# Two waves of Strassen products for 18 of the 25 column tiles of a decoder's input projection

## The chip, the cores and the metric

The kernel runs on one core of a Trainium2 chip. The metric is the device time in microseconds (us) of one execution, the median of several. A core has five engines that run side by side and wait for one another by semaphores: TensorE (PE, matmuls out of SBUF into the eight banks of PSUM), VectorE (DVE), ScalarE (ACT), GpSimd (POOL, which works on SBUF only) and SyncE (SP, which issues the transfers here).

## The reference

Two layers, for 1024 tokens of width 1024. Each layer is `h + mixer(norm(h))`, then `h + cross_attention(norm(h))`. The mixer begins with one projection of all tokens:

```
proj = xn @ w_in                 # (1024 x 1024) @ (1024 x 3168)
(gq, gk, gv, glr, ggate, cc, cb, ch, cgate, cq, ckv, kr, mgate) = split(proj)
o_gla  = rms_norm(gla_chunked(gq, gk, gv, log_a(glr)), gla_norm) * silu(ggate)
o_conv = cb * causal_conv3(cc * ch, conv_w) * silu(cgate)
q, k, v from rms_norm(cq) @ w_uq, rms_norm(ckv) @ w_ukv, rope(kr)
o_mla  = causal_attention(q, k, v) * silu(mgate)
return concat(o_gla, o_conv, o_mla) @ w_out
```

Everything is float32.

## The kernel before

Activations lie transposed: features on the partitions, tokens along the free dimension, in two halves c = 0, 1 of 512 tokens. So x is 8 (k) x 2 (c) tiles of 128 x 512. A float32 matmul is made of three in a shorter format: each operand is split into hi (a rounded cast, on ScalarE) and lo (the difference, on GpSimd or VectorE), and `mm3` (L298) adds hi x hi, hi x lo and lo x hi into one bank. `split` (L154) does that for activations, `wsplit` (L123) for weights; the subtraction of both is `sub` (L148), so all of them have the line L149 in the profile. `absorb` (L274) makes the parts of x as the layer before ends, and stores h in DRAM (`hd`).

`w_in` is cut into 25 tiles of 128 columns: 0 to 6 carry gq, gk and gv, 7 to 9 ggate, 10 to 17 the two halves of the conv (cc, ch, cb, cgate each), 18 and 19 cq, 20 and 21 ckv, 22 to 24 mgate. `win` (L393) loads one tile (512 KB), splits it, and for each half of the tokens makes 8 x 3 matmuls into one PSUM bank (`proj`, L305); VectorE multiplies the bank by `R`, the reciprocal norm of the tokens, into SBUF (L402). Gate tiles go through `silu` (L405) and to DRAM.

Memory is taken from pools of tagged buffers. The tag "s" has 64 granules of 128 x 512 float32, "pt" 4 and "p" 9; raw weight tiles ("wr") have 2 buffers, split ones ("w") 6. PSUM's eight banks are four with the tag S, two t, one mm and one v.

The kernel is written as generators that are advanced in a hand-made order (`layers`, L1143). A planner then simulates the engines and orders each queue: of what is ready and has its buffers it takes what was traced first. So the traced order is a priority, and work traced later can run earlier. Transfers all go through SyncE's one queue, in order. In a layer: tiles 0, 1, 2, 5 and 6 (gq, gk and the first v); `gla_front` (decays, L458) woven with the other v tiles and the first mgate; `v_tokens` (transposes of v, L443); `gla_body` (the recurrence) filled with the gates and the first conv; then ckv, cq, the second conv, rope and the attention; `out_proj`; the cross-attention.

Of the kernel before, what the change touches and what calls it, by code (L numbers as in the profile page):

```python
# [18 lines left out]
P = 128  # L19
# [41 lines left out]
def run(g):  # L61
# [4 lines left out]
BUFS = {"s": 64, "p": 9, "pt": 4, "tq": 1}  # L66
# [14 lines left out]
    "wk": (0, 2), "wv": (0, 2), "wq": (0, 2),  # L81
}


class Trunk:
# [330 lines left out]
    def gate(self, l, i, dram, name):  # L416

        gs = []

        def dst(c):  # L420
            gs.append(self.g(f"{name}_{c}", tag="pt"))
            return gs[-1]

        n = 0
        for _ in self.win(l, i, name, dst, PAIR[name[:2]]):
            self.silu(gs[n], f"{name}s_{n}")
            self.nc.sync.dma_start(dram[n], gs[n])
            n += 1
            yield

# [195 lines left out]
    def conv(self, l, j):  # L626
        nc = self.nc
        base = 10 + 4 * j
        tags = PAIR[f"conv{j}"]
        u = self.g2(f"cc{l}_{j}")  # L630
        y = self.g2(f"cy{l}_{j}")
        self.cy[j] = y
        yield from self.win(l, base, f"cc{l}_{j}", lambda c: u[c], tags)
        tmp = {}

        def dst(name):
            def f(c):
                tmp[c] = self.g(f"{name}{l}_{j}_{c}", tag="pt")
                return tmp[c]
            return f  # L640

        w = [self.gain(l, "conv", 2 * k + j) for k in range(3)]
        c = 0
        for _ in self.win(l, base + 1, f"ch{l}_{j}", dst("ch"), tags):
            self.mul(nc.gpsimd, u[c], u[c], tmp[c])
            nc.scalar.activation(y[c], u[c], AF.Copy, scale=w[2])
            for s in (1, 2):
                nc.vector.scalar_tensor_tensor(
                    y[c][:, s:], u[c][:, : 512 - s], w[2 - s], y[c][:, s:], op0=ALU.mult, op1=ALU.add
                )  # L650
                if c == 1:
                    nc.vector.scalar_tensor_tensor(
                        y[1][:, :s], u[0][:, 512 - s :], w[2 - s], y[1][:, :s], op0=ALU.mult, op1=ALU.add
                    )
            c += 1
            yield
        c = 0
        for _ in self.win(l, base + 3, f"cg{l}_{j}", dst("cg"), tags):
            self.silu(tmp[c], f"cgs{l}_{j}_{c}")
            self.mul(nc.gpsimd, y[c], y[c], tmp[c])  # L660
            c += 1
            yield
        c = 0
# [757 lines left out]
```

## Time and profile before

| | before |
|---|---|
| median of 3 runs (us) | 1416.54 (1415.16 to 1416.78) |
| profiled execution (us) | 1415.69 |
| its span, first to last instruction (us) | 1413.9 |
| granted TensorE clock, mean | 0.997 |
| busy: TensorE, VectorE, ScalarE, GpSimd (us) | 1382.9, 771.0, 690.0, 571.7 |
| moved by DMA | 131.13 MB, 93 GB/s on average |

The span is 1.8 us shorter than the time of that execution. Busy times are sums over instructions; those of one engine that overlap are counted once. A matmul's recorded time is longer than the distance to the next, since matmuls are pipelined: what one costs is read from the distance of their starts.

### The profile page before, as it was taken

How to read it: one execution, taken by the hardware profiler on the slowest of the kernel's cores; microseconds unless marked ns; L12 is line 12 of the kernel's file. 1: busy time of each engine (PE TensorE's matmuls, PEld its weight loads, DVE VectorE, ACT ScalarE, POOL GpSimd, SP SyncE). 2: the span in 40 equal slices, each digit the busy share in tenths (PEclk: the TensorE clock that was granted, in tenths of full speed). 3: DMA queues.
4: the chain of work that ended last, by engine and by line, in shares of the span. 5: the costliest groups of instructions: out<-in, count | busy, mean ns of one | idle time of the engine just before them, and what ended most of it. 6: DMA issues, size and time to landing. Idle time of an engine off the chain costs nothing.

```text
span 1413.9 us, 19744 instructions
## 1 busy us (share of the span) xinstructions
PE 1382.9 (98%) x7132; PEld 1128.0 (80%) x7132; DVE 771.0 (55%) x1431; ACT 690.0 (49%) x1462; POOL 571.7 (40%) x584
## 2 busy tenths in 40 slices
PE   7998999999999999999999999999999999999998
PEld 6787888888776688888878788888887767888886
DVE  7846445364788554545653632534657883553533
ACT  5446544253777442555431653424557773344543
POOL 6325335215556452353342532441356663414320
PEclk9999999999999999999999999999999999999999
DMA  8131222122122254321522121211232123534403
GB/s 310 53 129 53 77 76 74 47 63 91 45 61 65 92 172 134 121 89 46 185 100 82 49 78 53 89 58 45 83 86 60 33 81 112 194 105 142 156 1 120
DMA packets 61827, 131.13 MB, mean 93 GB/s; under 512 B 7553, under 2 KB 14497, under 8 KB 61729
## 3 DMA queue, kind: packets, MB, share of 16 engines
q1 hardware_dynamic: 61728, 129.87, 28.5%
q8 instruction: 56, 0.92, 0.3%
q14 instruction: 43, 0.34, 0.1%
HBM read 95.76 MB, written 33.55 MB: 91 GB/s over the span
## 4 chain that ended last, share of the span: by engine, by line
PE 83%; DVE 9%; ACT 3%; issue 2%; DMA 2%; POOL 1%; SPq 0%; DVEq 0%; POOLq 0%; ACTq 0%
PE op_ps L301 4%; PE op_ps L302 4%; PE op_ps L303 4%; PE av L848 4%; PE pt L834 3%; PE xqps L301 2%; PE xqps L302 2%; PE xqps L303 2%; PE s L301 2%; PE gg_ps L301 2%; PE gg_ps L303 2%; PE gg_ps L302 2%; PE s L303 1%; PE s L302 1%; DVE gla_a L479 1%
## 5 line engine op out<-in xcount | busy, mean ns | idle before, releaser
L149 POOL TENSOR_TENSOR win_l<-win_r,win_h 128x512 fp32r<-128x512 f32 x76 | 104.1, 1391 | 196.4 <-ACT win_h L127 191.6
L805 POOL TENSOR_SCALAR p<-p,sm 128x128 f32<-128x128 f32 (+3 forms) x144 | 87.8, 619 | 63.8 <-DVE sm L803 41.5
L127 ACT CAST win_h<-win_r 128x1024 fp32r<-128x1024 f32 x50 | 52.4, 1049 | 123.5 <-PE gg_ps L302 36.6
L303 PE MATMUL op_ps<-mix_h,wout_l 128*128 128x512 f32 x256 | 99.9, 390 | 0.0
L302 PE MATMUL op_ps<-mix_l,wout_h 128*128 128x512 f32 x256 | 99.8, 390 | 0.0
L301 PE MATMUL op_ps<-mix_h,wout_h 128*128 128x512 f32 x256 | 99.0, 393 | 0.0
L799 ACT ACTIVATE p<-s,nm 128x128 f32<-128x128 f32 (+3 forms) x144 | 83.2, 581 | 27.1 <-DVE nm L795 13.8
L791 DVE TENSOR_REDUCE nm<-s 128x1 f32<-128x128 f32 (+3 forms) x144 | 78.4, 551 | 3.1 <-PE s L303 1.1
L834 PE MATMUL pt<-ident,p 128*128 128x128 f32 x432 | 70.6, 280 | 1.6 <-POOL p L805 1.5
L834 PEld LDWEIGHTS pt<-ident,p 128*128 128x128 f32 x432 | 49.7, 140 | 27.3 <-issue 13.7
L848 PE MATMUL av<-ph,V 128*64 128x256 f32 x480 | 69.6, 375 | 0.0
L149 POOL TENSOR_TENSOR wout_l<-wout_r,wout_h 128x512 fp32r<-128x512 f32 x32 | 43.3, 1376 | 42.5 <-ACT wout_h L127 34.4
L301 PE MATMUL s<-k_h,q_h 128*128 128x128 f32 (+3 forms) x144 | 55.2, 386 | 1.3 <-ACT p L799 0.6
L301 PEld LDWEIGHTS op_ps<-mix_h,wout_h 128*128 128x128 f32 x256 | 47.7, 188 | 10.5 <-issue 0.8
L302 PEld LDWEIGHTS op_ps<-mix_l,wout_h 128*128 128x128 f32 x256 | 48.1, 188 | 9.9
L303 PEld LDWEIGHTS op_ps<-mix_h,wout_l 128*128 128x128 f32 x256 | 48.1, 188 | 9.8
L842 ACT COPY ph<-pt 128x512 f32<-128x512 f32 (+1 forms) x72 | 39.6, 549 | 23.7 <-PE pt L834 20.6
L301 PE MATMUL xqps<-op_x_h,wq_h 128*128 128x512 f32 x128 | 51.1, 399 | 0.0
L1005 POOL TENSOR_SCALAR xp<-xp,xsm 128x256 f32<-128x256 f32 x64 | 29.8, 482 | 51.4 <-DVE xsm L1003 51.3
L303 PE MATMUL xqps<-op_x_h,wq_l 128*128 128x512 f32 x128 | 50.4, 393 | 0.0
L302 PE MATMUL xqps<-op_x_l,wq_h 128*128 128x512 f32 x128 | 50.2, 392 | 0.0
L302 PE MATMUL s<-k_l,q_h 128*128 128x128 f32 (+3 forms) x144 | 49.9, 347 | 0.0
(502 smaller groups left out, 4292.5 us busy)
## 6 DMA issues: line engine op xcount, KB each, us to landing
win_r<-in_w_in SPq DMA_DIRECT2D x50, 512.0 KB, 3.6
wout_r<-in_w_out SPq DMA_DIRECT2D x16, 512.0 KB, 4.0
x<-in_x SPq DMA_DIRECT2D x16, 256.0 KB, 6.3
hd<-h SPq DMA_DIRECT2D x16, 256.0 KB, 4.0
op0r<-hd SPq DMA_DIRECT2D x16, 256.0 KB, 4.0
hd<-op0r SPq DMA_DIRECT2D x16, 256.0 KB, 2.9
wq_r<-in_w_mem SPq DMA_DIRECT2D x8, 512.0 KB, 3.8
wk_r<-in_w_mem SPq DMA_DIRECT2D x8, 512.0 KB, 3.6
```

The source lines that it names most:

```text
L127: ins = self.nc.scalar.copy(hi, raw)
L149: eng.tensor_tensor(lo, src, hi.bitcast(F32), op=ALU.subtract)
L301: nc.tensor.matmul(ps, a[0], b[0], start=first, stop=False, **k)
L302: nc.tensor.matmul(ps, a[0], b[1], start=False, stop=False, **k)
L303: nc.tensor.matmul(ps, a[1], b[0], start=False, stop=last, **k)
L791: nc.vector.tensor_reduce(nm[:, b : b + 1], ps[:, :w], axis=AX.X, op=ALU.max, negate=True)
L799: nc.scalar.activation(x[:, :w], ps[:, :w], AF.Exp, bias=nm[:, 0:1], accum_out=sm[:, b : b + 1])
L805: nc.gpsimd.tensor_scalar(pr[b][:, :w], pr[b][:, :w], sm[:, 0:1], 1.0, op0=ALU.mult, op1=ALU.mult)
L834: nc.tensor.transpose(ps[:, o : o + P], prob[qi][kt // 4][:, (kt % 4) * P : (kt % 4 + 1) * P], self.ident,)
L842: nc.scalar.copy(pt[:, :w], ps[:, :w])
L848: nc.tensor.matmul(av[own if j == 0 else other, q0:256], self.V[kt][:, 64 * h : 64 * h + 64], pt[:, j * 256 : j * 256 + 256 - q0], start=( ...
L1005: nc.gpsimd.tensor_scalar(pr[:, j], pr[:, j], sm[:, j : j + 1], 1.0, op0=ALU.mult, op1=ALU.mult)
```

## The change

18 of the 25 tiles of a layer are projected in nine pairs. With x cut into four quarters (the halves of the tokens by the halves of k, `half(j, c)`) and a pair of weight tiles cut into four as well, Strassen's method in Winograd's form gives the four quarters of the result from seven products of 4 x 3 matmuls in place of eight. It needs four sums of quarters of x (`a_side`: made anew from the stored h, the gains and R, stored in DRAM, later loaded and split by `s_parts`) and four of the weights (`w_first`, `w_second`). Wave one makes three products per pair with the x parts as they are, and stores two of the results (`pd`) and one weight sum (`wtd`); wave two makes the other four with the sums of x, and adds up. The parts of x are given up after wave one, and the sums take their place. The gate results of the conv go through DRAM too (`cgd`), the latents and the convs take their inputs from what wave two leaves (`Sink`, `GateSink`), and the order in `layers` is new. "s" has 58 granules, "pt" 6, and there are 4 raw weight buffers.

```diff
-BUFS = {"s": 64, "p": 9, "pt": 4, "tq": 1}
+BUFS = {"s": 58, "p": 9, "pt": 6, "tq": 1}
...
+    "sp": (0, 2), "wk": (0, 2), "wv": (0, 2), "wq": (0, 2),
...
+class GateSink(Sink):
...
+    def done(self, c):
+        self.k.silu(self.t[c], f"{self.name}s_{c}")
+        self.k.nc.sync.dma_start(self.dram[c], self.t[c])
...
+PAIRS = ((20, 21), (7, 18), (8, 19), (13, 10), (22, 11), (23, 12), (17, 14), (9, 15), (24, 16))
...
-        raw = self.wp.tile(shape, F32, tag="wr", bufs=2, name=name + "_r")
+        raw = self.wp.tile(shape, F32, tag="wr", bufs=4, name=name + "_r")
...
+    def a_side(self, l):
+
+        nc = self.nc
+        for k in range(4):
+            t = {}
+            for m, c in ((k, 1), (k + 4, 1), (k, 0), (k + 4, 0)):
+                x = self.g(f"sa{l}_{m}_{c}")
+                nc.sync.dma_start(x, self.hd[m][c])
+                nc.scalar.activation(x, x, AF.Copy, scale=self.gain(l, "mix", m))
+                self.mul(nc.gpsimd, x, x, self.R[c])
+                t[(m // 4, c)] = x
+            a11, a12, a21, a22 = t[(0, 0)], t[(1, 0)], t[(0, 1)], t[(1, 1)]
+            nc.vector.tensor_tensor(a22, a21, a22, op=ALU.add)
+            nc.gpsimd.tensor_tensor(a21, a11, a21, op=ALU.subtract)
+            nc.vector.tensor_tensor(a11, a22, a11, op=ALU.subtract)
+            nc.gpsimd.tensor_tensor(a12, a12, a11, op=ALU.subtract)
+            for j, x in enumerate((a22, a11, a21, a12)):
+                nc.sync.dma_start(self.sd[j][k], x)
+            yield
+
+    def s_parts(self, l, j):
...
+        for k in range(4):
+            raw = self.g(f"sr{l}_{j}_{k}", tag="pt")
+            nc.sync.dma_start(raw, self.sd[j][k])
+            hi, lo = self.g(f"sh{l}_{j}_{k}", F32R), self.g(f"sl{l}_{j}_{k}", F32R)
+            self.split(hi, lo, raw, eng=self.pick("sp", k))
+            self.Sp[j].append((hi, lo))
+            yield
+
+    def prod(self, ps, w, xs, first):
+        for k, x in enumerate(xs):
+            self.mm3(ps, w(k), x, first and k == 0, k == len(xs) - 1, skip_group_check=True)
+
+    def w_first(self, l, n):
...
+        r1, r2 = raws
+        hi, lo = self.wsplit(r1, sh, f"win{l}_{i1}")
+        nc.gpsimd.tensor_tensor(r2[:, :4], r2[:, :4], r1[:, :4], op=ALU.subtract)
+        nc.gpsimd.tensor_tensor(r2[:, 4:], r2[:, 4:], r2[:, :4], op=ALU.subtract)
+        t4 = self.g(f"t4_{l}_{n}", tag="tq", shape=[P, 4, P])
+        nc.vector.tensor_tensor(t4, r1[:, 4:], r2[:, 4:], op=ALU.subtract)
+        nc.sync.dma_start(self.wtd[n], r2)
+        w4 = self.wp.tile(sh, F32R, tag="w", bufs=6, name=f"w4_{l}_{n}")
+        nc.scalar.copy(w4[:, :4], t4)
+        self.sub(nc.vector, w4[:, 4:], t4, w4[:, :4])
...
+    def w_second(self, l, n):
...
+        t12 = self.wraw(self.wtd[n], sh, f"t12_{l}_{n}")
+        r2 = self.wraw(self.A["w_in"][l, i2].rearrange("p (k c) -> p k c", k=KT), sh, f"win2_{l}_{i2}")
+        (nc.vector if n % 2 else nc.gpsimd).tensor_tensor(r2[:, :4], r2[:, 4:], r2[:, :4], op=ALU.subtract)
...
+        for j, r in enumerate((t12, r2)):
...
+            nc.scalar.copy(hi, r)
+            for h in (0, 4):
+                self.sub(nc.vector if j and h else nc.gpsimd, lo[:, h : h + 4], r[:, h : h + 4], hi[:, h : h + 4])
...
+    def wave1(self, l, order):
...
+            self.prod(x, wb, a11, True)
+            p1 = self.g(f"p1_{l}_{n}", tag="pt")
+            nc.vector.tensor_tensor(p1, x, self.R[0], op=ALU.mult)
+            nc.sync.dma_start(self.pd[n][0], p1)
+            yield
+            if at + 1 < len(order):
+                w = self.w_first(l, order[at + 1])
+            self.prod(y, w4, a22, True)
...
+            self.prod(x, lambda k: wb(4 + k), a12, False)
+            s = self.sink[PAIRS[n][0]]
+            nc.vector.tensor_tensor(s.tile(0), x, self.R[0], op=ALU.mult)
+            s.done(0)
...
+    def wave2(self, l, order):
...
+            t1, t2, t3, b22 = self.w_second(l, n)
+            p = [self.g(f"pl{l}_{n}_{i}") for i in range(2)]
+            for i in range(2):
+                nc.sync.dma_start(p[i], self.pd[n][i])
+            tags = ("S", "S") if at % 2 else ("mm", "t")
...
+            self.prod(x, t2, s2, True)
+            nc.vector.tensor_tensor(u2, x, p[0], op=ALU.add)
+            yield
+            if at == 0:
+                self.prod(x, t3, s3, False)
+                self.prod(y, t1, s1, True)
+            else:
+                self.prod(y, t1, s1, True)
+                self.prod(x, t3, s3, False)
+            nc.scalar.copy(y5, y)
+            nc.vector.tensor_tensor(u3, x, p[0], op=ALU.add)
+            yield
+            k1, k2 = (self.sink[i] for i in PAIRS[n])
+            nc.gpsimd.tensor_tensor(k2.tile(1), y5, u3, op=ALU.add)
+            (nc.gpsimd if n % 2 else nc.vector).tensor_tensor(k1.tile(1), u3, p[1], op=ALU.add)
+            k1.done(1)
+            self.prod(y, b22, s4, False)
+            nc.vector.tensor_tensor(k2.tile(0), y, u2, op=ALU.add)
...
+            first = self.wave1(l, (4, 5, 1, 2, 7, 8, 3, 6, 0))
+            values = chain(*(self.in_v(l, f, PAIR["gv"]) for f in (1, 2)), first)
...
+            for i in range(8):
+                next(fronts)
+                if i < 7:
+                    next(values)
+                if i % 2 == 0:
+                    next(sides)
...
+            for r in range(4):
                 for b in bodies:
                     next(b, None)
-                    for _ in range(2):
-                        next(fill, None)
+                    if r:
+                        next(parts, None)
+                        next(parts, None)
+                    for _ in range(3):
+                        next(first, None)
...
+            self.after = {
+                2: chain(self.latent(l, "ckv", 20), self.latent(l, "cq", 18)),
+                5: self.conv(l, 0),
+            }
...
+            second = self.wave2(l, range(9))
+            for _ in range(21):
+                next(second)
             self.wkn = self.mla_w(l, 2)
...
             run(self.krope(l))
+            run(second)
             run(self.mla_k(l, 0))
             run(conv)
             run(self.mla(l))
```

## Rows read from the trace of the kernel before

**Rows 1.** The page: busy us, share, instructions; the clock in 40 slices.

```profile
PE 1382.9 (98%) x7132; PEld 1128.0 (80%) x7132; DVE 771.0 (55%) x1431; ACT 690.0 (49%) x1462; POOL 571.7 (40%) x584
...
PEclk9999999999999999999999999999999999999999
```

**Rows 2.** The page: the chain that ended last, by engine.

```profile
PE 83%; DVE 9%; ACT 3%; issue 2%; DMA 2%; POOL 1%; SPq 0%; DVEq 0%; POOLq 0%; ACTq 0%
```

**Rows 3.** Busy time of each engine by stretch; the first line names the columns.

```profile
core 0: us, PE busy (x) PEld busy (x) DVE busy (x) ACT busy (x) POOL busy (x), PEclk, DMA share, GB/s
66.00:137.00 71.00, 66.54 (x310) 55.12 (x308) 41.31 (x61) 39.68 (x75) 27.31 (x25) 0.98 0.28 95
...
66.00:345.00 279.00, 273.81 (x1323) 229.88 (x1322) 134.66 (x210) 127.19 (x234) 99.00 (x83) 0.99 0.23 75
345.00:480.00 135.00, 133.53 (x810) 97.31 (x809) 107.25 (x297) 95.76 (x257) 83.48 (x111) 1.00 0.23 64
...
752.00:1031.00 279.00, 275.65 (x1322) 231.12 (x1322) 124.28 (x195) 121.52 (x219) 98.34 (x83) 0.99 0.21 66
```

**Rows 4.** Chain of waits, 96 to 128 us; then TensorE's timeline behind it.

```profile
100.16 1.30 POOL gla_b L476
...
116.35 2.24 DVE gla_a L479 x2
...
126.89 0.49 ACT gv L453
...
127.42 1.28 PE L449 MATMUL gvt<-ident,vf 128*128 128x128 f32 x6 [4.46 <-ACT gv L453]
128.35 0.78 PE L301 MATMUL mg_ps<-h_x_h,win_h 128*128 128x512 f32 x1
...
131.37 0.40 PE L302 MATMUL mg_ps<-h_x_l,win_h 128*128 128x512 f32 x1
```

**Rows 5.** The matmuls of ckv's tiles: ns min/median/max, first and last start in us.

```profile
L301 PE MATMUL ckv_ps<-h_x_h,win_h x32: 389/389/393, 251.5 to 272.6; 128*128 128x512 f32 x32
```

**Rows 6.** Single groups: ns min/median/max; last two: busy us, mean ns, idle before.

```profile
L152 POOL TENSOR_TENSOR mg<-mg,mg_0s x4: 1275/1290/1292, 121.3 to 813.7; 128x512 f32<-128x512 f32 x4
...
L402 DVE TENSOR_TENSOR mg<-mg_ps,h_acc x6: 677/682/692, 109.2 to 153.6; 128x512 f32<-128x512 f32 x6
...
L149 DVE TENSOR_TENSOR win_l<-win_r,win_h x24: 667/685/960, 69.2 to 983.9; 128x512 fp32r<-128x512 f32 x24
...
L127 ACT CAST win_h<-win_r 128x1024 fp32r<-128x1024 f32 x21 | 22.0, 1048 | 36.9 <-PE gg_ps L302 18.3 <-PE ch_ps L302 4.1 <-PE ckv_ps L302 3.8
...
L409 ACT ACTIVATE cgs<-cg 128x512 f32<-128x512 f32 x4 | 2.5, 632 | 0.8 <-DVE cg L402 0.6
```

**Rows 7.** GpSimd's and VectorE's timelines, 116 to 123 us; L484's durations.

```profile
116.38 3.30 POOL L149 TENSOR_TENSOR win_l<-win_r,win_h 128x512 fp32r<-128x512 f32 x2 [0.58 <-ACT win_h L127]
119.64 1.75 POOL L152 TENSOR_TENSOR gk<-gk,gla_a 128x512 f32<-128x512 f32 x1
121.34 1.29 POOL L152 TENSOR_TENSOR mg<-mg,mg_0s 128x512 f32<-128x512 f32 x1
...
121.45 1.46 DVE L484 TENSOR_TENSOR gla_a<-gla_a,tot 128x256 f32<-128x256 f32 x1
...
L484 DVE TENSOR_TENSOR gla_a<-gla_a,tot x8: 424/426/1475, 104.1 to 808.7; 128x256 f32<-128x256 f32 x8
```

**Rows 8.** The page's DMA issues: KB each, median us to landing.

```profile
op0r<-hd SPq DMA_DIRECT2D x16, 256.0 KB, 4.0
...
mgd<-mg SPq DMA_DIRECT2D x12, 256.0 KB, 2.0
```

**Rows 9.** SyncE's queue: start us, us, transfers.

```profile
25.03 1.18 SPq L217 DMA_DIRECT2D posi<-in_positions  x2
...
57.52 13.37 SPq L120 DMA_DIRECT2D win_r<-in_w_in  x3
70.98 1.81 SPq L368 DMA_DIRECT2D mem<-in_mem  x4
```

More of the change, by code (lines that the diff above doesn't have):

```diff
@@ new lines, in wave1 @@
+    def wave1(self, l, order):
+        nc = self.nc
+        half = lambda j, c: [(self.x1[4 * j + k][0][c], self.x1[4 * j + k][1][c]) for k in range(4)]
+        a11, a12, a22 = half(0, 0), half(1, 0), half(1, 1)
+        w = self.w_first(l, order[0])
+        for at, n in enumerate(order):
+            tags = ("S", "S") if at % 2 else ("mm", "S")
+            x = self.psum(tags[0], f"wx{l}_{n}")
+            y = self.psum(tags[1], f"wy{l}_{n}")
+            wb, w4 = w
+            self.prod(x, wb, a11, True)
[6 more added lines that the diff above has]
+            self.prod(y, w4, a22, True)
+            p4 = self.g(f"p4_{l}_{n}", tag="pt")
+            nc.vector.tensor_tensor(p4, y, self.R[1], op=ALU.mult)
+            nc.sync.dma_start(self.pd[n][1], p4)
+            yield
[4 more added lines that the diff above has]
+            yield
@@ new lines, in wave2 @@
+    def wave2(self, l, order):
+        nc = self.nc
+        s1, s2, s3, s4 = (self.Sp[j] for j in range(4))
+        for at, n in enumerate(order):
+            t1, t2, t3, b22 = self.w_second(l, n)
[3 more added lines that the diff above has]
+            tags = ("S", "S") if at % 2 else ("mm", "t")
+            x = self.psum(tags[0], f"vx{l}_{n}")
+            y = self.psum(tags[1], f"vy{l}_{n}")
+            u2, u3 = self.g2(f"u{l}_{n}")
+            y5 = self.g(f"y5_{l}_{n}")
+            self.prod(x, t2, s2, True)
[9 more added lines that the diff above has]
+            nc.vector.tensor_tensor(u3, x, p[0], op=ALU.add)
+            yield
+            k1, k2 = (self.sink[i] for i in PAIRS[n])
[4 more added lines that the diff above has]
+            nc.vector.tensor_tensor(k2.tile(0), y, u2, op=ALU.add)
+            k2.done(0)
+            k2.done(1)
+            yield
+            if n in self.after:
+                yield from self.after[n]
@@ new lines, in sinks @@
+    def sinks(self, l):
+        self.sink = {}
+        for i in range(3):
+            self.sink[22 + i] = GateSink(self, self.mgd[i], f"mg{l}_{i}")
+            self.sink[7 + i] = GateSink(self, self.ggd[i], f"gg{l}_{i}")
+        for j in range(2):
+            self.sink[13 + 4 * j] = GateSink(self, self.cgd[j], f"cg{l}_{j}")
+            for i in range(3):
+                self.sink[10 + 4 * j + i] = Sink(self, f"c{i}{l}_{j}")
+        for i in range(18, 22):
+            self.sink[i] = Sink(self, f"lat{l}_{i}")
@@ L672, in latent @@
         nc = self.nc
-        raw = [self.g2(f"{what}{l}_{i}") for i in range(2)]
+        raw = [self.sink[base + i].t for i in range(2)]
         acc = self.g2(f"{what}acc{l}", tag="pt")
         for i in range(2):
-            c = 0
-            for _ in self.win(l, base + i, f"{what}{l}_{i}", lambda c: raw[i][c], PAIR[f"lat{i}"]):
+            for c in range(2):
                 if i == 0:
@@ L683, in latent @@
                     nc.vector.tensor_tensor(acc[c], acc[c], sq, op=ALU.add)
-                c += 1
-                yield
+        yield
         parts = [self.parts(f"{what}p{l}_{i}") for i in range(2)]
@@ L1187, in layers @@
             self.qp = [None] * HEADS
+            self.after = {
+                2: chain(self.latent(l, "ckv", 20), self.latent(l, "cq", 18)),
+                5: self.conv(l, 0),
+            }
             conv = self.conv(l, 1)
-            run(self.latent(l, "ckv", 20))
-            run(self.latent(l, "cq", 18))
+            second = self.wave2(l, range(9))
+            for _ in range(21):
+                next(second)
             self.wkn = self.mla_w(l, 2)
-            for _ in range(2):
-                next(conv)
             run(self.krope(l))
+            run(second)
             run(self.mla_k(l, 0))
```

116 lines of the change are left out of this document (66 added, 50 removed).

## The prediction

> **What bounds the kernel now.** Read first the busy times and the clock [rows 1]: TensorE is busy 1382.9 of 1413.9 us, and its granted clock stays at the upper of its two levels (2.4 GHz) in every slice but for short relapses. The next engine, VectorE, has 55%. The chain that ended last agrees: 83% of it is TensorE [rows 2]. So a matmul taken out is worth its spacing, as long as the others keep up. Then the stages [rows 3]: the projection work after the first tiles (66 to 345 us in layer 0, 752 to 1031 in layer 1) has 273.8 and 275.7 us of TensorE in 279, with VectorE at 134.7, ScalarE at 127.2 and GpSimd at only 99.0. Inside it TensorE idles in layer 0 for 4.5 us between 66 and 137 and for 0.7 us after that, in layer 1 for 3.4.
>
> That one idle place matters. From 96 to 127 us the chain of waits is not TensorE but the fronts of the linear attention: ScalarE, GpSimd and VectorE by turns, until the transposes of v wait 4.46 us for a ScalarE copy [rows 4]. The seven matmuls after it are 0.43 us apart instead of 0.23, the lower level (1.2 GHz): such a stall costs about 7 x 0.2 = 1.4 us more.
>
> **What is removed.** A pair of tiles takes 2 x 2 x 24 = 96 matmuls; seven products of 12 take 84. Nine pairs in two layers save 9 x 12 x 2 = 216. The spacing comes from one group: 32 starts in 21.1 us, so 93 matmuls, 0.227 us each [rows 5]. 216 x 0.227 = 49.0 us, 24.5 per layer. Nothing is added on TensorE. The profiled execution took 1415.7 us, its span and 1.8 us around it; with no new idle time that would become 1366.7.
>
> **What is added, per layer.** GpSimd: the A sums take 24 operations (16 products, 8 differences), the splits of the four sums 8 of 16, wave one 4 per pair (36), wave two 3 or 4 per pair (32), the last sums 13; 13 of the old 18 tiles had 26 there. Net 113 - 26 = 87 at 1.29 us [rows 6], 112 us, so 211; less six of the second conv that now come after the stretch (7.7), 203. The stretch that TensorE needs is 279 - 24.5 = 254.5 us: GpSimd goes from 35% to 80%. VectorE: 8 + 8 + 18 + 13 + 5 new two-operand operations, 10 old ones gone, 54 evacuations and sums out of PSUM for 36: +60 at 0.69 us [rows 6] is 41, so 176, 69%. ScalarE: 16 scalings and 16 casts of 512 columns (0.63 us), half a cast less per pair in wave one, two casts of 1024 columns (1.05 us) and one copy per pair in wave two [rows 6]: 10 + 10 - 4 + 19 + 5 = 40, so 167, 66%. Each alone fits.
>
> **They do not run alone.** When both work on SBUF operands, one waits for the other [rows 7]: a VectorE operation that takes 0.43 us took 1.46, and GpSimd operations of 1.29 took 1.65 and 1.75. An evacuation, one operand in PSUM, is never over 0.69 [rows 6]. So a collision costs GpSimd up to 0.46 and VectorE up to 1.05 us. By the code some 85 VectorE operations of the stretch read two SBUF operands now; with 42 more, some 125. If all collide, GpSimd needs 203 + 125 x 0.46 = 260 us of 254.5; if none does, 203. No row shows TensorE full beside such a load (the attention, full but for 1.5 us in 135, has GpSimd at 62% [rows 3]), so I cost what is late by place.
>
> The Trainium skill has a rule against the change here ("SBUF — State Buffer", section "SBUF: two separate sides"): the port pair that the two engines share is locked for the whole instruction, and the loser blocks. The blocking agrees with [rows 7]; that GpSimd pays the whole 0.69 us doesn't. By the rule the sum would be 203 + 125 x 0.69 = 289 us a layer, 35 over TensorE's, and the kernel 20 us slower.
>
> *Up to the recurrence (66 to 137).* TensorE's work is 66.5 us, with 84 matmuls of wave one for 72 of two gates, 69. GpSimd had 27.3; the A sums bring 31, the weights of three pairs 15.5 for 2.6: 71 before collisions. They fall into the very chain of [rows 4], whose some 20 VectorE operations can each lose 1.05 us. Against that, the A sums are wanted only by wave two and need only the norm and the stored h. Work traced later does run earlier where a buffer is free: the positions of the rotary tables are loaded at 25 us, ahead of the memory tokens at 71 that are traced before them [rows 9]. Bounds 0 and 20 us; nearest to the 4.5 idle now, I take 6.
>
> *From wave one to wave two.* The first pair needs the second sum at once, the third after 12 matmuls, the first right behind it, the fourth after 36. The splits of two sums come only as x's parts leave: 8 loads, 8 casts, 4 GpSimd and 4 VectorE operations, some 8 us on ScalarE and GpSimd side by side, part of it under the last products of wave one. Bounds 0 and 10, taken 2.5.
>
> *In wave two.* A pair is 48 x 0.227 = 10.9 us of TensorE; GpSimd has 5.9 operations, 7.6 us, VectorE 5.9, 4.1 us, and once both latents (24 on VectorE) and a conv. A bank is read and then added to again: the next product on it must wait for the evacuation, and only one product of 12 (2.7 us) lies between, where before a bank had a tile's whole 24. A VectorE operation that collides just ahead eats 1.05 of that. Granules are short as well: the sums hold 32 of 58, the latents' parts 16, a pair's own p, u and y5 take 5, so from the fifth pair the conv's inputs use up the rest; late next is y5's copy, then the last product. Bounds 0 and 15, taken 4.
>
> *Later.* The second conv runs beside the first attention tiles; x's new parts and the mixer's parts together are 64 granules, so with 58 the last split waits for the first half of the last output tile, and some q parts for old ones. That is covered by the last tile's 24 matmuls (5.4 us). Bounds 0 and 8, taken 1.5.
>
> *Transfers.* 92 of 256 KB and 27 of 512 KB a layer, 38 MB more on 21: some 230 GB/s, which by 0.23 of the engines at 75 GB/s [rows 3] is 0.7 of them. Those of 256 KB land in 2 to 4 us now [rows 8]. SyncE's queue gets 119 issues more at 0.33 us, 39 us: it fits. But one issue that waits holds all behind it: three loads stood 13.4 us for a weight buffer, ahead of the memory tokens [rows 9]. Four raw buffers loosen that; the stores of p1, p4 and the sums put new waits in. I put nothing for it beyond the bounds above.
>
> **The sum.** 6 + 2.5 + 4 + 1.5 = 14 us of new idle a layer, 28 in all, against 49.0: 1415.7 - 21 = 1394.7, the profiled execution being 0.85 under the median of the three runs: 1395.5 us.
>
> **Rivals.**
> 1. *Clean* (chance 0.17): the order hides the sums and the stalls stay under 5 us a layer, 1367 to 1378. For it: full TensorE in all of the stretch but one place [rows 3]; against: [rows 4] and the 80%.
> 2. *GpSimd and its collisions become the bound* (0.21). The first part then lasts its 71 + 39 collisions (25 there now, 14 new) x 0.46 = 89 us for TensorE's 69, wave two 80 (the pairs 69, one conv 7.7, latent weights 4) + 60 x 0.46 = 108 us for 101, and two relapses of the clock are 2.8: 30 us a layer, 60 - 49 = 11 slower, 1427. It decides from 24.5 us of idle a layer. For it: [rows 7]; against: the A sums can wait, and many of the operations fall where the other engine idles. The rule above is its extreme, 1436.
> 3. *What is saved is just given back* (0.08): the short granules and the single queue cost 24 us a layer through loads that come late by a landing each (4 us [rows 8], for six of the nine pairs); 1414 to 1419. Against: loads of a pair depend on nothing but old stores and a buffer.
>
> The forecast has 0.54, on its own 1378 to 1413. 0.2% (2.8 us) is about what a measurement here can tell from no change. Faster by more: forecast and rival 1, 0.71; within: 0.08; slower: 0.21. The range goes from the clean end, 1369, to 1430, past rival 2; the rule's 1436 stays outside.
>
> **What would show it.** TensorE's matmuls fall by 216 with their spacing unchanged, so its busy time by some 49 us. GpSimd is at 75 to 85% between 66 and 325. TensorE idles most before the recurrence, less where wave two begins, then in short pieces that end on VectorE or ScalarE. I am wrong on the low side if GpSimd's A sums stand early, or late behind the fronts; on the high side if TensorE waits for win_l or w4 in wave one, or for pd loads in wave two, pair after pair.

## The result and the profile after

The changed kernel takes 1533.92 us (median of four runs, 1530.44 to 1537.42) against 1416.00 (1415.16 to 1416.78): 1.083 times as long, 95% interval 1.081 to 1.086. The forecast was 1395.5 and the range ended at 1430. The profiled execution, the slowest of the four (1537.42 us), has a span of 1535.5 us, 121.6 more than before; all stages below are read from it.

The page, busy times and the clock in 40 slices [rows 1]:

```profile
PE 1394.7 (91%) x6916; PEld 1116.0 (73%) x6916; DVE 930.0 (61%) x1551; ACT 761.8 (50%) x1580; POOL 832.2 (54%) x758
...
PEclk9997899988999999999999989997899999999999
```

The matmuls fell by 216, as the change says, yet TensorE is busy 12 us longer, and idle 140.8 us (1535.5 - 1394.7) instead of 31.0. The clock's mean fell from 0.997 to 0.955: some 138 us at 1.2 GHz (2 x 0.045 x 1535.5; called half-clock time below), against some 8.

Busy time by stretch, columns as in [rows 3]. In each layer: from the first decay matmul to the last transpose of v, the rest of wave one, wave two, and the attention (that of layer 0 alone).

```profile
core 0: us, PE busy (x) PEld busy (x) DVE busy (x) ACT busy (x) POOL busy (x), PEclk, DMA share, GB/s
...
99.40:161.00 61.60, 39.77 (x167) 32.12 (x166) 46.16 (x43) 36.98 (x65) 52.93 (x43) 0.82 0.48 162
161.00:252.70 91.70, 83.77 (x436) 71.41 (x435) 64.17 (x94) 45.52 (x91) 63.50 (x48) 0.94 0.71 239
252.70:399.00 146.30, 121.56 (x476) 94.93 (x476) 78.92 (x94) 64.84 (x105) 91.55 (x66) 0.90 0.40 130
399.00:537.00 138.00, 128.70 (x748) 92.97 (x747) 107.69 (x294) 95.95 (x254) 84.40 (x110) 0.98 0.25 70
844.20:901.00 56.80, 44.14 (x193) 34.83 (x192) 45.65 (x45) 37.93 (x67) 50.46 (x40) 0.91 0.49 167
901.00:990.00 89.00, 80.93 (x438) 68.51 (x436) 69.00 (x93) 44.44 (x93) 70.27 (x53) 0.98 0.68 234
990.00:1141.00 151.00, 125.33 (x475) 97.16 (x476) 77.31 (x97) 64.73 (x105) 91.01 (x66) 0.88 0.41 131
```

Wave two has 476 matmuls. At 0.227 us they need 108 us; it takes 146 and 151, while no other engine is busy more than 63% of it. That alone is 38 and 43 us a layer. Of this, 24.7 and 25.7 us are idle time; the other 13.5 and 17.5 are TensorE busy for longer than 0.227 us a matmul, at a granted clock of 0.90 and 0.88. The first stretch is 21 and 12 us longer than before (41.2 and 45.4 by the same matmuls), and GpSimd is busy 86 and 89% of it.

What TensorE waited for: the whole run by kinds of wait (us in total, times, longest).

```profile
PE gvt L633 <- ACT gv L637: 17.0, 4, 10.9
PE vx L335 <- DVE u L579: 13.9, 8, 3.7
PE wx L335 <- DVE p L548: 11.1, 3, 8.6
PE cq_ms L296 <- ACT cq_ah L193: 9.5, 4, 4.7
...
PE vy L335 <- ACT y L587: 7.8, 4, 2.5
...
PE vx L335 <- ACT w2h L525: 5.3, 4, 1.8
```

In wave two there is no one wait but a different one for each product. Its timeline, TensorE and what it waited for (start, us, line, operands, idle before):

```profile
317.30 0.40 PE L337 MATMUL vy<-sh,w2l 128*128 128x512 f32 x1
319.45 0.65 PE L335 MATMUL vx<-sh,w2h 128*128 128x512 f32 x1 [1.76 <-ACT w2h L525]
319.90 0.63 PE L336 MATMUL vx<-sl,w2h 128*128 128x512 f32 x1
320.33 0.63 PE L335 MATMUL vy<-sh,w2h 128*128 128x512 f32 x1
...
326.42 0.39 PE L337 MATMUL vx<-sh,w2l 128*128 128x512 f32 x1
...
326.75 1.05 ACT L525 CAST w2h<-win_r 128x1024 fp32r<-128x1024 f32 x1 [2.81 <-PE vx L336]
327.04 0.69 DVE L579 TENSOR_TENSOR u<-vx,pl 128x512 f32<-128x512 f32 x1 [1.21 <-DMA pl<-pd]
...
327.79 0.50 PE L335 MATMUL vx<-sh,w2h 128*128 128x512 f32 x1 [0.98 <-DVE u L579]
328.13 0.39 PE L336 MATMUL vx<-sl,w2h 128*128 128x512 f32 x1
328.36 0.40 PE L337 MATMUL vx<-sh,w2l 128*128 128x512 f32 x1
...
333.15 0.39 PE L337 MATMUL vy<-sh,w2l 128*128 128x512 f32 x1
335.43 0.57 ACT L587 COPY y<-vy 128x512 f32<-128x512 f32 x1
...
336.05 0.50 PE L335 MATMUL vy<-sh,w2h 128*128 128x512 f32 x1 [2.51 <-ACT y L587]
```

Read upward from each wait: a product waits for its weights' cast; a sum (`u`) waits for the loaded p1 (`pl`), which comes late (short granules are a part of that, as e5 shows below); the last product waits for y5's copy, which starts 2 us after its product ended. Behind the first gap the matmuls are 0.43 us apart (319.90, 320.33), the lower level; at 328.13 and 328.36 they are 0.23 apart again.

In layer 0's first stretch the sums of x lie in the fronts of the linear attention:

```profile
151.53 7.43 POOL L186 TENSOR_TENSOR sa<-sa,h_acc 128x512 f32<-128x512 f32 x6
...
152.75 6.76 DVE L446 SCALAR_TENSOR_TENSOR mg_1s<-mg,mg_1s 128x512 f32<-128x512 f32 x1 [7.33 <-ACT mg_1s L445]
...
159.54 0.63 ACT L447 ACTIVATE mg_1s<-mg_1s 128x512 f32<-128x512 f32 x1 [5.03 <-DVE mg_1s L446]
...
160.19 0.48 ACT L637 COPY gv<-gvt 128x384 f32<-128x384 f32 x1
...
160.72 0.90 PE L633 MATMUL gvt<-ident,vf 128*128 128x128 f32 x3 [5.62 <-ACT gv L637]
```

A VectorE operation that takes 0.69 us undisturbed (the same on another gate, at 336.64 us) stands 6.76 us while GpSimd runs six multiplications of the sums; ScalarE waits for it, and `gv` and TensorE behind ScalarE.

**Where the time went, by stages.** The table gives the distances of the starts of named TensorE matmuls (z: first decay matmul; v: last transpose of v; vx, vy: first and last of wave two; s: first score; o: first of the output projection), in us, layer 0 / layer 1, with the time and the mean clock of each kernel.

```
kernel              time     clock  z to v       v to vx      vx to vy       vy to s      s to o
before              1416.00  0.997  41.2/45.4    (v to s: 214.7/214.7)                    118.7/118.7
after               1533.92  0.955  61.8/57.3    91.5/88.6    146.1/150.6    8.4/8.4      129.7/128.8
e2 keys late        1523.34  0.966  61.7/56.9    89.1/89.4    138.3/145.9    9.4/9.4      128.5/128.8
e3 eight weights    1534.77  0.963  57.2/55.6    91.5/90.7    147.9/149.8    7.9/7.9      129.5/129.6
e4 no sums          1475.96  0.974  45.2/48.8    78.7/78.2    141.1/142.3    8.2/8.5      128.7/129.4
e5 sums in p        1509.87  0.964  61.8/57.1    89.9/88.7    135.1/135.6    8.4/8.4      128.8/129.3
e6 sums later       1519.47  0.965  45.0/48.2    94.5/91.6    148.6/151.3    8.3/8.4      128.8/129.1
e7 three moves      1486.68  0.970  45.0/49.6    93.2/90.6    128.8/131.5    13.2/13.3    127.6/127.7
e8 more GpSimd      1540.24  0.957  61.8/57.4    90.2/85.7    152.3/149.7    8.1/8.1      131.0/130.3
e9 conv spread      1533.53  0.961  61.9/57.5    90.7/86.6    142.9/151.3    7.4/7.4      131.5/129.1
e10 sums on vector  1507.82  0.962  59.5/65.8    78.3/77.5    142.6/143.2    8.4/8.3      128.8/128.8
e11 all moves       1484.80  0.973  45.2/49.7    88.7/92.9    131.8/126.6    16.9/13.3    126.7/126.7
e12 fillers         1528.72  0.973  61.8/56.8    91.3/87.8    146.2/146.1    8.9/8.8      126.9/127.7
e13 no sums, moved  1454.89  0.982  45.3/49.7    78.2/77.4    129.5/131.5    13.2/13.3    126.7/126.7
e14 fillers, moved  1486.17  0.981  45.0/48.5    90.7/91.8    139.6/135.6    8.5/8.5      126.6/125.8
e15 one weight      1445.48  0.981  45.0/48.5    88.1/88.9    120.4/120.6    7.3/7.3      127.7/127.6
e16 early keys      1483.21  0.970  45.0/48.9    88.1/93.5    145.5/140.0    -8.5/-7.8    136.5/135.8
e17 neither         1426.06  0.985  45.4/49.7    77.3/76.5    121.7/120.8    7.3/7.3      128.3/128.3
```

Of the 121 us, 51.8 and 44.8 lie between z and s of the two layers (though 24.5 was taken out of each), 11.0 and 10.1 in s to o, 3.8 ahead of layer 0's z; from layer 0's o to layer 1's z, and after layer 1's o, both kernels need the same (307.3 and 251.2). Each experiment was timed once; the runs of the changed kernel lie within 7 us of one another, so differences of about 5 us say nothing.

### The profile page after: what moved, and what is told of

It reads as the page before. It is cut to its first block, busy times and chain, and to the rows that moved or that the text cites. A ratio compares the mean times of both kernels' runs of the same rounds, so it can differ in the third digit from the quotient of the medians.

```text
span 1535.5 us, 20397 instructions
## 1 busy us (share of the span) xinstructions
PE 1394.7 (91%) x6916; PEld 1116.0 (73%) x6916; DVE 930.0 (61%) x1551; ACT 761.8 (50%) x1580; POOL 832.2 (54%) x758
## 5 line engine op out<-in xcount | busy, mean ns | idle before, releaser
L183 POOL TENSOR_TENSOR win_l<-win_r,win_h 128x512 fp32r<-128x512 f32 x60 | 88.7, 1498 | 53.9 <-ACT win_h L161 49.1
L335 PE MATMUL vx<-sh,w2h 128*128 128x512 f32 x144 | 64.3, 446 | 25.2 <-DVE u L579 13.9
L183 POOL TENSOR_TENSOR w2l<-t_r,w2h 128x512 fp32r<-128x512 f32 x36 | 50.6, 1424 | 40.9 <-ACT w2h L525 40.9
L335 PE MATMUL vy<-sh,w2h 128*128 128x512 f32 x144 | 59.9, 420 | 7.8 <-ACT y L587 7.8
L337 PE MATMUL vy<-sh,w2l 128*128 128x512 f32 x144 | 59.9, 420 | 3.7 <-POOL w2l L183 3.7
L336 PE MATMUL vx<-sl,w2h 128*128 128x512 f32 x144 | 62.0, 430 | 0.0
L337 PE MATMUL vx<-sh,w2l 128*128 128x512 f32 x144 | 61.7, 428 | 0.0
L336 PE MATMUL vy<-sl,w2h 128*128 128x512 f32 x144 | 60.0, 417 | 0.0
L335 PEld LDWEIGHTS vx<-sh,w2h 128*128 128x128 f32 x144 | 30.9, 214 | 38.3 <-DVE u L579 11.0
L161 ACT CAST win_h<-win_r 128x1024 fp32r<-128x1024 f32 x32 | 33.4, 1045 | 49.8 <-PE gq_ps L336 22.8
```

The lines of the kernel that those rows point to most:

```text
L161: ins = self.nc.scalar.copy(hi, raw)
L183: eng.tensor_tensor(lo, src, hi.bitcast(F32), op=ALU.subtract)
L335: nc.tensor.matmul(ps, a[0], b[0], start=first, stop=False, **k)
L336: nc.tensor.matmul(ps, a[0], b[1], start=False, stop=False, **k)
L337: nc.tensor.matmul(ps, a[1], b[0], start=False, stop=last, **k)
```

## The experiments

**Buffers alone.** The kernel before, with the sizes of the changed one:

```diff
-BUFS = {"s": 64, "p": 9, "pt": 4, "tq": 1}
+BUFS = {"s": 58, "p": 9, "pt": 6, "tq": 1}
-tag="wr", bufs=2
+tag="wr", bufs=4
```

> The kernel before with nothing but the new buffer counts (58 granules, 6 pt, 4 raw weight buffers). If the short granules lengthen the attention stage (118.7 to 129.7 us in layer 0, 118.7 to 128.8 in layer 1), this kernel shows the same +10 us per layer there and takes about 1436 us. If the second conv that now lies beside the first attention tiles does it, the time stays within 3 us of 1416.

1414.66 beside 1416.78 on the same chip. The smaller pool costs 2 us in each attention (120.8 and 120.9 from s to o) and nothing on the whole.

**Where the split weights are held up.** In e2 the key weights of the attention, two of the six split-weight buffers, are loaded behind wave two:

```diff
-            self.wkn = self.mla_w(l, 2)
             run(self.krope(l))
             run(second)
+            self.wkn = self.mla_w(l, 2)
             run(self.mla_k(l, 0))
```

> The changed kernel, the weights for the attention's keys (two of the six split-weight buffers, held until the last keys) loaded behind wave two and not inside it. Theory buffers: wave two is set by split weights that wait for a buffer, worst in its second half, where the pairs have 4 buffers; wave two (146 and 151 us) loses 12 to 25 us per layer and the time is 1485 to 1510. Theory GpSimd and its collisions: the same operations in the same number, wave two within 5 us, the time within 10 us of 1534.

1523.34: 10.6 us less. Wave two is 7.8 and 4.7 us shorter, and 1.0 us a layer comes back ahead of the scores: between the two theories.

In e3 there are eight split-weight buffers (`w` 6 to 8) and, to fit, two raw ones (`wr` 4 to 2).

> The changed kernel with 8 split-weight buffers in place of 6, paid for by 2 raw ones in place of 4. Theory buffers: the next pair's weights can be split a pair ahead, wave two falls from 146 to 150 us to some 120, the time to about 1480, less what the two lost raw buffers cost. If it is the raw weights and the queue of transfers that come late, it gets slower than 1534. Theory GpSimd: within 10 us of 1534.

1534.77, no change. As raw buffers were taken away for it, this doesn't clear the weights; e15 does it better.

**The sums of x.** e4 leaves them out: wave two takes the plain quarters of the stored h in place of the sums, so its products are of other numbers. The loads and splits of the parts stay.

```diff
-            nc.sync.dma_start(raw, self.sd[j][k])
+            nc.sync.dma_start(raw, self.hd[k + 4 * (j % 2)][j // 2])
-            sides = self.a_side(l)
+            sides = iter(())
```

> The changed kernel without the sums of x: the 24 GpSimd, 8 VectorE and 16 ScalarE operations and the 64 transfers per layer of that step are left out, and wave two takes plain h in their place. Theory GpSimd and its collisions for the stretch before the recurrence: from the first decay matmul to the last transpose of v it goes from 61 and 57 us back to the 41 to 45 of before, and the time falls by 30 to 45 us to 1490 to 1505; wave two stays as it is, within 5 us. If that stretch is late for the new weight work instead, it stays within 5 us of 61 and 57.

1475.96, 58 us less, the largest single item (the transfers left out are 32 a layer; the 64 above are of both). From z to vx the layers lose 29.4 and 18.9 us, wave two 5.1 and 8.3.

e6 keeps the sums but traces them in the first half of the recurrence, out of the fronts:

```diff
                 if i < 7:
                     next(values)
-                if i % 2 == 0:
-                    next(sides)
...
-                    if r:
+                    if r < 2:
+                        next(sides)
+                    if r == 1 and b is bodies[1]:
+                        run(sides)
+                    if r > 1:
```

> The changed kernel with the sums of x made in the first half of the recurrence and not between the decay fronts; the splits of the sums begin in its second half. Same work. If the sums cost time because they stand in the chain of the fronts, the stretch up to the last transpose of v falls from 61 and 57 to about 45 us and wave one, with GpSimd at 70%, takes up a part: the time is 1495 to 1515. If they cost it as plain GpSimd time wherever they stand, wave one grows by what the first stretch loses and the time is within 10 us of 1534.

1519.47. The first stretch is as short as without the sums (45.0 and 48.2), but wave one behind it is 16 and 13 us longer than in e4: of the 48 us that the sums cost between z and vx, 28 move on with them.

e10 does the sums' 24 GpSimd operations a layer on VectorE:

```diff
-                self.mul(nc.gpsimd, x, x, self.R[c])
+                self.mul(nc.vector, x, x, self.R[c])
-            nc.gpsimd.tensor_tensor(a21, a11, a21, op=ALU.subtract)
+            nc.vector.tensor_tensor(a21, a11, a21, op=ALU.subtract)
-            nc.gpsimd.tensor_tensor(a12, a12, a11, op=ALU.subtract)
+            nc.vector.tensor_tensor(a12, a12, a11, op=ALU.subtract)
```

> The changed kernel with all 24 operations of the sums of x that GpSimd made per layer (16 multiplications, 8 differences) on VectorE. Theory: the run of GpSimd operations one behind another keeps VectorE out, and that is what stalls the fronts; then the stretch from the first decay matmul to the last transpose of v falls from 61 and 57 us to 45-52, and the time by 10 to 20 us. Rival: it is the plain amount of work in the fronts, whoever does it; then VectorE, 75% busy there, takes 24 operations more (some 17 us) and the stretch stays over 57 us.

1507.82, 26 us less, but not as the theory had it. The long stand of `mg_1s` is gone (columns: busy us, mean ns, idle before it; 10.8 us and 2690 ns on average in the changed kernel):

```profile
L446 DVE SCALAR_TENSOR_TENSOR mg_1s<-mg,mg_1s 128x512 f32<-128x512 f32 x4 | 4.0, 1004 | 0.0
```

Yet z to v is 59.5 and 65.8: 2 us shorter in one layer, 9 longer in the other, as the rival had it. The gain is in wave one, 13 and 11 us. VectorE is now nearly full in the first stretch (94 and 95%; the first window ends where the last run of transposes begins), as GpSimd was in the changed kernel (86 and 89%: 52.93 of 61.60 and 50.46 of 56.80 us above; time in which an operation stands counts as busy):

```profile
98.20:154.70 56.50, 38.78 (x154) 30.55 (x153) 53.21 (x63) 37.21 (x63) 37.40 (x28) 0.83 0.64 223
824.10:889.70 65.60, 50.30 (x196) 39.82 (x194) 62.62 (x75) 39.32 (x70) 38.02 (x30) 0.82 0.56 203
```

So the stretch is long with the sums on either engine, and as short as without them where they are moved out (e4, e6): it is the sums' work beside the fronts that makes it long. As e10 takes the long stand away and fills VectorE at once, it does not show what the stand alone costs. On VectorE the moved operations take 0.96 to 1.21 us each on average, on GpSimd 1.34 to 1.43.

**Granules in wave two.** e5 takes a pair's five (`pl` x2, `u2`, `u3`, `y5`) from the nine of the pool p, and not from s:

```diff
-            p = [self.g(f"pl{l}_{n}_{i}") for i in range(2)]
+            p = [self.g(f"pl{l}_{n}_{i}", tag="p") for i in range(2)]
-            u2, u3 = self.g2(f"u{l}_{n}")
-            y5 = self.g(f"y5_{l}_{n}")
+            u2, u3 = self.g2(f"u{l}_{n}", tag="p")
+            y5 = self.g(f"y5_{l}_{n}", tag="p")
```

> The changed kernel, with the five granules that each pair of wave two needs (two loaded products, u2, u3, y5) taken from the tag p, whose 9 buffers are idle there, and not from the 58. Theory granules: wave two (146 and 151 us) is set by pairs that wait for the granules of the pair before, so it falls to 115 to 125 us and the time to 1470 to 1485. Theory queue (the loads come late behind other transfers) and theory GpSimd: wave two within 8 us, the time above 1515.

1509.87, 24 us less; wave two 135.1 and 135.6, so 11 and 15 shorter. Short granules were a third of its excess over 108, not all. The sums' waits for `pl` fell from 8.7 to 4.6 us and TensorE's for y5's copy from 7.8 to 2.8; neither vanished.

**GpSimd in wave two.** e8 gives GpSimd the 18 operations a layer on weights and on k1 that VectorE has there:

```diff
-        (nc.vector if n % 2 else nc.gpsimd).tensor_tensor(r2[:, :4], ...
+        nc.gpsimd.tensor_tensor(r2[:, :4], ...
-                self.sub(nc.vector if j and h else nc.gpsimd, lo[:, h : h + 4], ...
+                self.sub(nc.gpsimd, lo[:, h : h + 4], ...
-            (nc.gpsimd if n % 2 else nc.vector).tensor_tensor(k1.tile(1), ...
+            nc.gpsimd.tensor_tensor(k1.tile(1), ...
```

> The changed kernel with all weight and sum operations of wave two that VectorE has (18 per layer) on GpSimd, 23 us more of GpSimd work per layer there. Theory GpSimd: wave two grows by 15 to 23 us per layer, 1565 to 1580. Theory granules: GpSimd is idle for 55 of 146 us there, so it grows by at most 8 per layer, below 1550.

1540.24: 6 us more, within the spread, for 36 operations of 1.29 us in the two layers, 46 us of work. GpSimd's throughput is not what sets wave two.

**Moves together.** e7 is e2, e5 and e6 at once.

> The changed kernel with the pair's granules in p, the sums later and the key weights behind wave two. If the three costs are apart, the gains add up: 1534 less some 60, 30 and 10, 1425 to 1445, still above the 1416 of before. If one takes the place of another, it stays above 1460.

1486.68, 47 us less: close to the sum of the three (10.6 + 24.0 + 14.5 = 49.1), but above what was expected of the first theory. Wave two keeps 129 and 132 us.

**The clock.** e12 puts 12 matmuls more into each pair but the wave's first, into the idle bank v, which nothing reads (192 in all, not 216 as the expectation has it; 43.6 us at 0.227):

```diff
                 self.prod(y, t1, s1, True)
+                self.filler(f"f0{l}_{n}", t1, s1)
                 self.prod(x, t3, s3, False)
...
             k1.done(1)
+            if at:
+                self.filler(f"f1{l}_{n}", t3, s3)
             self.prod(y, b22, s4, False)
...
+    def filler(self, name, w, xs):
+        ps = self.psum("v", name)
+        for k, x in enumerate(xs[:2]):
+            self.mm3(ps, w(k), x, k == 0, k == 1)
```

> The changed kernel with 12 matmuls more per pair of wave two, into a bank that nothing reads, six ahead of the third product and six ahead of the last: 216 in all, 49 us at 0.227. Theory of the clock: the gaps between the products are what drops the granted clock, and matmuls that wait for nothing fill the gaps and hold the clock up; then the half-clock time falls from 139 us to under 100, and the time stays at or under 1534 although 216 matmuls are added. Rival: TensorE's work sets the time there and the clock does not follow from these gaps; then 1550-1583.

1528.72, not slower with 192 matmuls more. Wave two of both layers (columns as above):

```profile
253.00:399.20 146.20, 134.28 (x567) 107.25 (x567) 78.17 (x95) 65.62 (x106) 92.54 (x66) 0.96 0.42 135
986.80:1133.00 146.20, 135.28 (x566) 108.03 (x567) 76.58 (x97) 65.44 (x105) 91.18 (x66) 0.96 0.43 139
```

The granted clock there went from 0.90 and 0.88 to 0.96, half-clock time on the whole from 138 to some 82 us, so the gaps do drop it. But wave two did not grow: the fillers' 21.8 us a layer went into idle time (from 25 and 26 us to 12 and 11) and into what the other matmuls gained at full speed (8 and 11 us). That fits a stage set by waits, where the low clock follows from them. It does not show what the clock alone is worth, since the fillers stand in TensorE's own queue and may hold up a product that is ready.

**The second conv.** e9 advances its steps behind the first attention tiles, not ahead of them:

```diff
-            run(conv)
-            run(self.mla(l))
+            run(self.mla(l, conv))
...
             yield from self.mla_tail(l, h, ip)
+            if n:
+                next(conv, None)
```

> The changed kernel, but the four steps of the second conv are traced behind the first four attention tiles, not ahead of them. Theory: the second conv beside the first attention tiles is what made the attention 10 us longer per layer; then the stretch from its first score matmul to its first output projection falls from 129 to 119-122 us and the time to 1513-1520. Rival: the attention is longer because its fronts start cold behind wave two (no stock of q and k made ahead); then it stays within 2 us of 129 and the time within 5 us of 1534.

1533.53, s to o 131.5 and 129.1. The theory fell.

**All moves.** e11 is e7 with the edits of e9 and e10.

> The three moves together (the five granules of a pair in the tag p, the sums made in the recurrence, the key weights behind wave two), and besides the second conv spread over the attention and the sums' operations on VectorE. If what is left is waits that these two edits touch (the sums beside the recurrence, the attention), 1450-1475; if it is the chain of a pair inside wave two with the clock's relapses, 1480-1490. Not below 1416 by either.

1484.80, no better than e7 and within its second range. The next four are edits of e11. e13 leaves the sums of x out as e4 did:

> All moves, with the sums of x left out (wave two takes the plain quarters of the stored h in their place, so the results of the pairs are other numbers). If the sums are what still holds wave one and the start of wave two, wave one falls from 89 and 93 us to 79 and the time to 1455-1465; if they hold wave two as well (the DMA of 16 MB, the granules), wave two falls below 120 from 132 and 127 and the time to under 1445. If neither, over 1475.

1454.89, 29.9 less, nearly all between v and vx (78.2 and 77.4). Wave two moved both ways, 2 us down and 5 up.

e14 puts the fillers of e12 into e11:

> All moves, with 12 matmuls more in each of eight pairs a layer of wave two, into a bank that nothing reads: 192, 43.6 us at 0.227. If wave two is set by the chain of the other engines, the fillers go into its gaps: wave two stays at 127-135 us and the time at 1475-1495, with less half-clock time than 82 us. If TensorE is what sets it by now, wave two grows by 22 us a layer and the time to 1520-1530.

1486.17. Wave two grew by 8 and 9 us, somewhat more than expected, and the scores stood 8 and 5 us nearer behind it. From vx to s the layers need 148.1 and 144.1 us for e11's 148.6 and 139.9, so most of the 21.8 us of fillers a layer went into time in which TensorE had stood or run at the lower clock.

e15 makes wave two's weights once a layer and uses them for all nine pairs. It leaves out the loads, sums, casts and differences of the other eight.

```diff
-            t1, t2, t3, b22 = self.w_second(l, n)
+            if at == 0:
+                t1, t2, t3, b22 = self.w_second(l, n)
```

> All moves, with wave two's weights loaded, summed and split once a layer and used for all nine pairs (left out: the weights of the other eight). If the chain of the weights holds wave two, it falls from 132 and 127 us to 110-116 and the time by 25 to 40 us, to 1445-1460. If it is the evacuations and what follows them, wave two stays over 122 us and the time over 1472.

1445.48, 39.3 less. Wave two of e11 and, in the second fence, of e15, both layers:

```profile
232.70:364.40 131.70, 114.50 (x467) 90.63 (x467) 80.79 (x93) 64.41 (x105) 86.45 (x63) 0.92 0.46 146
958.60:1085.20 126.60, 112.20 (x468) 88.92 (x467) 80.39 (x93) 63.89 (x105) 88.92 (x63) 0.95 0.46 151
```

```profile
230.70:351.10 120.40, 111.50 (x484) 89.95 (x483) 59.94 (x86) 51.23 (x94) 53.41 (x40) 0.96 0.31 104
930.60:1051.20 120.60, 111.21 (x484) 89.70 (x483) 58.52 (x85) 51.72 (x94) 54.61 (x40) 0.96 0.32 103
```

GpSimd has 54 us in place of 87, and the stage is 11 and 6 us shorter, with the scores 9.6 and 6.0 us nearer behind it (the first key products now lie 28 us ahead of wave two's end, in e11 7). Transfers, casts and differences fall together here (the DMA share from 0.46 to 0.31), so the run doesn't show which of them counts. The stage falls between the two theories, the time as the first had it. What TensorE still waits for in it is mostly the latents' norms (7.4 and 7.9 us in the two layers); the longest waits of layer 0:

```profile
276.16 0.49 PE L296 MATMUL ckv_ms<-ckv_ah,ones 128*128 128x512 f32 x1 [2.00 <-ACT ckv_ah L193]
...
283.44 0.79 PE L296 MATMUL cq_ms<-cq_ah,ones 128*128 128x512 f32 x1 [3.61 <-ACT cq_ah L193]
```

e16 traces the first keys and queries behind pair 7, so that the last pair's products lie beside them:

```diff
                 5: self.conv(l, 0),
+                7: self.early(l),
...
+    def early(self, l):
+        self.wkn = self.mla_w(l, 2)
+        yield from self.krope(l)
+        yield from self.mla_k(l, 0)
+        for h in range(2):
+            yield from self.mla_q(l, h)
```

> All moves, with the rotary part of the keys, the first two heads' keys and the first two heads' queries traced behind pair 7 of wave two, so that the last pair's products lie beside them. If the attention is long because nothing covers its first fronts, the way from the end of wave two to the first score falls from 17 and 13 us to under 6, the attention from 127 to 119-122, wave two grows by the 7 us of the matmuls moved into it, and the time falls by 15 to 30 us, to 1455-1470. If the fronts are long for another reason, the time stays within 6 us of 1484.8.

1483.21. The scores now start 8 us ahead of wave two's end, but from vx to o the layers need 273 and 268 us for e11's 275 and 267: the work changed places. The theory of uncovered first fronts fell too.

e17 leaves out both the sums of x and the other pairs' weights:

> All moves, with the sums of x left out and wave two's weights made once a layer (the two omissions of the last runs together). If the two costs are separate, 1484.8 - 29.9 - 39.3 = 1415.6, within 6 us; if they are one and the same shortage (the engines beside the products), over 1428.

1426.06, between the two theories. The two share 10.5 us; together they hold 58.7 of the 118 us that e11 has over 1366.7.

## Why the prediction was wrong

**What held.** 216 matmuls went, at 0.227 us at full clock (328.13 to 328.36 above, as in [rows 5]). The transfers grew by 76.6 MB, 38 a layer as reckoned, and their share was 0.40 in wave two, 0.71 at most in the stages above. GpSimd's work was sized well: 221.6 us between 66 and 399 us, against 203 without and 260 with all collisions. (As a share it was 65% between 66 and 325 us, 169.3 of 259, and not the 75 to 85 forecast, since the stretch grew under it.) The rule of the Trainium skill that stood against the change ("SBUF — State Buffer", section "SBUF: two separate sides") gave 289 for it. The trace has less: in that time GpSimd operations of 1.29 us took 1.85 at the most. The places were named rightly: the fronts, y5's copy, granules, the weights' reloads.

**The step that failed** is the sum: "6 + 2.5 + 4 + 1.5 = 14 us of new idle a layer". From z to o a layer should have fallen by 24.5 us, to 350.2 and 354.3; it took 437.4 and 433.8. That is 87 and 79 us over, six times the 14.

1. *Wave two*, "bounds 0 and 15, taken 4", with 2.5 for the hand-over: it measured 38 and 43, of them 25 and 26 idle. I priced it by busy time (a pair has 10.9 us of TensorE, 7.6 of GpSimd, 4.1 of VectorE) and let one product of 2.7 us cover one evacuation. But a pair is a chain across a load, a cast, two differences, a product, a sum with a loaded granule, a copy and the next product, and links of it hold buffers that the next pair wants. e5 gives 11 and 15 of it to the granules; e2 8 and 5 to the two split-weight buffers held for the keys, of which 1 comes back ahead of the scores; after these moves e15 gives 11 and 6 to the weights' loads, sums and splits together. Some 12 us over 108 are left there, of which TensorE waits 7 to 8 for the latents' norms. GpSimd's throughput was not the matter (e8), and VectorE and ScalarE were less busy still (54 and 44%).
2. *Up to the recurrence*, "bounds 0 and 20; I take 6". The sums cost 29 and 19 us from z to vx (e4), and in the recurrence still 16 and 13 (e6 against e4). I reckoned that they would run early, since they need only the norm and h. They did not: their first load was issued at 98.0 us, one step of the sums by two of the fronts as traced, and none was moved ahead. And "a collision costs VectorE up to 1.05" was a bound for one operation, where a run of six cost 6.07 (6.76 less 0.69). In layer 0's first stretch that stand ended in a wait of TensorE of 5.6; what it costs apart from the sums' work is open (e10).
3. *Later*, 1.5: it measured 8.4 from vy to s, where before no such gap stood alone, and 11 and 10 in the attention. 2 of these are the smaller pool (e1). e9 and e16 tried the second conv and the uncovered first fronts, and both failed. In e11 TensorE is at full clock there but idle 7.5 us in many short waits. What makes them is not settled.
4. *The clock*, two relapses of 1.4 us a layer in a rival: 138 us at the lower level, some 130 more than before, so a loss of up to 65 us if it were a cost of its own. In wave two slow matmuls are 13.5 and 17.5 us of the 38 and 43. e12 speaks for a consequence of the waits there and doesn't settle what it costs by itself.

None of the rivals was right as a whole. The second (GpSimd and collisions as the bound, 1427) had the sign, and its first term, 89 us for 69 up to the recurrence, is about what came: that stretch grew by 21 and 12 us with GpSimd at 86 and 89% of it. So the forecast's 6 was the worse price of the two there. Its wave two, 108 for 101, was as far off as the forecast's, and e8 speaks against its mechanism there. The third, buffers and loads that come late, is nearer in kind to wave two, but had 24 us a layer. Nor did TensorE idle most before the recurrence: in wave two it was as much in layer 0 and twice that in layer 1 (24.7 and 25.7 us against 21.8 and 12.7, by the stretches above).

Of the 167 us over the clean 1366.7, the five moves take 49, the sums and the weights left out another 59, and 59 stand even then: about 13 a layer in wave two, 7 between it and the scores, 9.6 in the attention. With these two left out as well, e17 still takes 10 us longer than the kernel before. No version tried that computes all of it came under 1483.

## What to carry to other kernels

Price a stage that is cut into short dependent pieces by its chain and by the buffers that each link holds, not by each engine's share of the whole stage: in wave two no engine but TensorE was over 63% busy, and TensorE lost a quarter of the stage. A share over many stages hides a short one that is full: GpSimd had 65% between 66 and 325 us and 86% in the first stretch. A kernel with TensorE at 98% has its preparation hidden behind long uniform runs of matmuls; a change that takes matmuls out and puts preparation in takes away the cover as well, as here up to the recurrence; so ask for every new operation which matmuls lie beside it. Matmuls that nobody needs, put in the gaps, show in one run whether the gaps lower the clock; what the clock costs by itself they don't show.

## What the runs showed of the hardware

A VectorE operation with two SBUF operands stood while six GpSimd operations ran one behind another (151.53 to 158.96; it began at 152.75 and ended at 159.51), and not just for one: [rows 7] had shown 1.05 us at the most. The reverse is there too: at 53.45 us a GpSimd operation of 1.29 us took 2.63 beside two VectorE operations in a row with two SBUF operands (53.65 to 54.93).

The lower clock came again and again behind short idle times. After 1.76 us without a matmul the next ones were 0.43 us apart, after 0.98 us only one distance was longer (0.34), and then 0.23 again. The Trainium skill tells of a kernel whose clock goes back and forth through small idle times between groups of matmuls ("TensorE: Matmul & The Clock Gate", section "A second HAM failure mode: psum-queue depth-cycling"). The trace agrees as to the clock (0.88 to 0.90 in wave two). That the throughput suffers by it, as is said there, no run here shows apart: e12 raised the clock to 0.96 with matmuls that nobody needs, and the stage stayed at 146 us.
